# Other step clocks, weights loaded behind x, and small work moved between engines in a one-core S5 and gated-DeltaNet block

## The chip, the cores and the metric

The kernel runs on one core of a Trainium2 chip. Every time is in microseconds (us) of device time for one execution of the whole program. The time of a kernel is the median of its runs. The engines of the core are TensorE (PE, with its weight loads as PEld), VectorE (DVE), ScalarE (ACT), GpSimd (POOL) and SyncE (SP), which issues nearly all DMA transfers. Each works through its own instructions in program order and waits on the others by semaphores.

## The reference

One decoder block for 1024 tokens of width 1024, all in float32:

```
a = rms_norm(h, norm_mix_g)
u_s, z_s, q, k, v, z_d, b_raw, a_raw = split(a @ w_in)
y_s = s5_branch(u_s, ...) * silu(z_s)          # 32 groups, 64 states, gelu, then the GLU:
                                               # y * sigmoid(y @ w_glu + b_glu)
y_d = gated_deltanet_branch(q, k, v, z_d, b_raw, a_raw, ...)
                                               # causal conv of 4 taps + silu on q, k, v;
                                               # l2 norms of q, k; 4 heads of 128, chunks of 64
                                               # g = -exp(A_log) * softplus(a_raw + dt_bias)
h = h + concat(y_s, y_d) @ w_out
e = rms_norm(p @ w_ple_proj, ple_norm_g)
h = h + sigmoid(h @ w_ple_gate) * e
out = rms_norm(h, final_norm_g)
```

The chunk rule solves a unit lower triangular system per chunk and head; the output is the last RMS norm.

## The kernel before

**Products.** A float32 matrix is split into a high and a low part (`hi` is a rounded copy, `lo = raw - hi`, function `split`); a product is three matmuls, hi by hi, hi by lo and lo by hi (`mm3`). The split of a weight is one ScalarE copy (`wh`) and one subtraction, on VectorE for `w_in`'s tiles (`wl`) and by default on GpSimd.

**Stages.** In the prologue the squares of x are taken on ScalarE (`square`) and summed by scans on VectorE (`sumsq`); `rms` is a chain of some fifty small VectorE operations; `scale_x` multiplies the eight row tiles of x by the result. Meanwhile `e_proj` computes the 16 tiles of p @ w_ple_proj (PSUM tile `pe`), which ScalarE evicts to `e`. `xprep` transposes one 128-column slice of half of x on TensorE (`xtp`, four transposes) and evicts it as `ah` (ScalarE) and `al` (VectorE). From then on `inproj` multiplies one weight tile after another by both halves of x (`half`, PSUM tile `pj`, 24 matmuls each). Beside it run the a-chain (`a_prefix`: the prefix sums of the a gate by matmuls against `tg` and `dg`, PSUM tile `pT`, and scans on VectorE), and four batches of S5: `prep` builds `s5x`, TensorE transposes it (`hp`), ScalarE copies that out (`s5h`), TensorE makes the kernels (`kps`), the state injections (`inj`) and, after a scan, the outputs (`yps`). Then come the gate math with the softplus (`g_math`), the transposed v rows (`vtp`, scaled into `vr`), the decay matrices, a forward substitution on VectorE (`subst`), the doubling of the 32-row inverses to 64 (`double`, with `q32`, `d32`, `q64`, `d64`; printed as q and d), the GLU of S5 (`glu`, PSUM tile `pg`; `gr` is y loaded again, `gh` and `gl` its parts), eight chunks of the recurrence (`chunk`, PSUM tile `bk`), and at last the output projection and the gate (`po`, `pq`).

**What sets the order.** TensorE's order is planned by the program itself (the loop behind `fillers`, from line 1419): a clock counts the matmul time issued so far, and each chain (`x_chain`, `a_chain`, `s5_chain` and others) says with a `yield` how much of that clock has to pass before its next step. These numbers stand in the tables `LAT` (line 470) and `PL` (line 1344). Where no chain is due, fillers are issued in the order of the string `FILL`: u, b, q, k, gates, v, z, then the GLU and the outputs. The order on the other engines follows from the same program and the scheduler. Only one raw weight buffer (`wr`) exists, so a weight is loaded when the split of the one before is done. Loads that SyncE issues run one after another from one queue: p and w_ple, x, small tables (`pk`, `wba`, `hb`, `ldt`), and then the weights.

Of the kernel before, what the change touches and what calls it, by code (L numbers as in the profile page):

```python
# [8 lines left out]
F32 = mybir.dt.float32  # L9
# [7 lines left out]
P = 128  # L17
# [8 lines left out]
def hymba_block_kernel(ctx: ExitStack, tc: tile.TileContext, A: dict, out: bass.AP, dbg=None):  # L26
# [149 lines left out]
    xt_ = []  # L176
# [84 lines left out]

    def e_proj(i):
        t, nh = (i % 4, i // 4) if i < 8 else (i // 2, i % 2)
        p = MM("pe")
        for k in range(2):
            (ph, pl), (wh_, wl_) = ew["pt"][k], ew["wp"][k]
            mm3(p, ph[:, csl(t)], pl[:, csl(t)], wh_[:, hsl(nh)], wl_[:, hsl(nh)], k == 0, k == 1)
        yield 0
        if t in (5, 6):
            e = T2("e")  # L270
            act(e, p, AF.Copy)
            SP.dma_start(out=ed[t][:, hsl(nh)], in_=e)
# [11 lines left out]
        xload(i)  # L284
    SP.dma_start(out=pk, in_=A["pk"])
    SP.dma_start(out=wba, in_=A["wba"])

    ah = [T(f"ah{k}", F32R) for k in range(8)]
    al = [T(f"al{k}", F32R) for k in range(8)]

    def xprep(k, hf):
        p = MZ("xtp", [P, 4, P])
        for i in range(4):
            x4 = xt_[4 * hf + i].rearrange("p (c t j) -> p j c t", j=4, c=2)
            tr(p[:, i, :], x4[:, k // 2, k % 2, :], ident)
        hs = hsl(hf)
        g = pk[:, 126 + k:127 + k]
        act(ah[k][:, hs], flat(p), AF.Copy, scale=g)
        return stt(V, al[k][:, hs], flat(p), g, ah[k][:, hs].bitcast(F32), MUL, SUB)

    def scale_x():
        for i in range(8):
            r = ts(V, xt_[i], xt_[i], rinvs[:, i:i + 1], MUL)
        return r

    ctx.enter_context(tc.manual_schedule(engines={mybir.EngineType.PE}))
    e_split("pt", 0)
# [4 lines left out]
        square(i)  # L312
        sumsq(i)
    rms()
    scale_x()
    for i in range(16):
        for _ in e_proj(i):
            pass
# [50 lines left out]
    def s5_params():  # L369
# [98 lines left out]
    kpv = kp.rearrange("h (b j q) t -> b q j h t", j=4, q=2)  # L468

    LAT = dict(  # L470
        prep=14.1, ev=3.3, scan=18.0, tab=6.0, g1=23.0, g2=4.0, dec=14.8, sub=25.0, blk=0.3,
        q32=6.9, d32=8.0, q64=2.0, d64=0.8, kq=4.3, A=1.4, B=4.8, C=1.4, otp=10.3, vtp=23.2, ssq=30.3,
        bs8=11.4, gl=15.1, par=13.8, xp=1.2, sse=1.5, ql=14.0,
    )
    s5t = {}
# [6 lines left out]
    def s5_batch(b):  # L482
# [27 lines left out]
        for ri in range(2):  # L510
# [1 line left out]
            for j in range(4):  # L512
                tr(p[:, j, :], flat(ab[:, ri, j]), ident)
            act(h[:, ri], p, AF.Copy)
        yield LAT["ev"]
        kt = W("x1", "p (q c) -> p q c", c=P)
        kps = [f("kps")[:, 0:P] for f in (MS, MZ)]
        for ri in range(2):
# [79 lines left out]
    def wtile(mt):  # L598
        lo = wp.tile([P, 8, P], F32R, tag="wl", name="wl")
        hi = wp.tile([P, 8, P], F32R, tag="wh", name="wh")  # L600
        raw = raw_w([P, 8, P])
        SP.dma_start(out=raw, in_=A["win"][mt].rearrange("p (k c) -> p k c", k=8))
        split(hi, lo, raw, S, V)
        return hi, lo

    def half(w, hf, evac):
# [151 lines left out]
    def g_math():  # L758
# [40 lines left out]
        lp, lq, l2, lx, lx3, la, lb, lc = (V36()[:, 0:32] for _ in range(8))
        ts(V, lp, ee, 4.527000055531971e-05, MUL)  # L800
        for c in (0.4985410273075104, 6.578732490539551, 29.91191864013672, 60.949668884277344, 57.11296463012695):
            stt(V, lp, lp, c, ee, ADD, MUL)
        ts(V, lp, lp, 20.039552688598633, ADD)
        V.tensor_copy(out=lq, in_=ee)
        for c in (15.062909126281738, 83.04756927490234, 221.7624053955078, 309.0987243652344, 216.42788696289062):
            stt(V, lq, lq, c, ee, ADD, MUL)
        ts(V, lq, lq, 60.11865997314453, ADD)
        V.reciprocal(out=lq, in_=lq)
        tt(V, lp, lp, lq, MUL)
        tt(V, l2, ee, ee, MUL)  # L810
        tt(V, lq, ee, l2, MUL)
        tt(V, lp, lq, lp, MUL)
        stt(V, lp, l2, -0.5, lp, MUL, ADD)
        tt(V, lp, ee, lp, ADD)
        ts(V, lx, ee, 1.0, ADD, 0.5, MUL)
        ts(V, lx, lx, -1.0, ADD)
        tt(V, l2, lx, lx, MUL)
        tt(V, lx3, l2, lx, MUL)
        ts(V, la, lx, 0.07037683576345444, MUL)
        stt(V, la, la, -0.11514610052108765, lx, ADD, MUL)  # L820
        stt(V, la, la, 0.11676998436450958, lx3, ADD, MUL)
        ts(V, lb, lx, -0.12420140951871872, MUL)
        stt(V, lb, lb, 0.14249323308467865, lx, ADD, MUL)
        stt(V, lb, lb, -0.16668057441711426, la, ADD, ADD)
        tt(V, lb, lb, lx3, MUL)
        ts(V, lc, lx, 0.2000071406364441, MUL)
        stt(V, lc, lc, -0.24999994039535522, lx, ADD, MUL)
        stt(V, lc, lc, 0.3333333134651184, lb, ADD, ADD)
        tt(V, lc, lc, lx3, MUL)
        ts(V, lc, lc, -0.00021219444170128554, ADD)  # L830
        stt(V, l2, l2, -0.5, lx, MUL, ADD)
        tt(V, lc, l2, lc, ADD)
        ts(V, lc, lc, 0.693359375, ADD)
        ts(V, la, ee, 0.4142135679721832, ALU.is_lt)
        ts(V, lb, la, -1.0, MUL, 1.0, ADD)
        tt(V, lp, lp, la, MUL)
        tt(V, lc, lc, lb, MUL)
# [117 lines left out]
    def v_tile(h):  # L955
        if not vr:
            vr.extend(T(f"vr{c}", F32, [P, 2, 4, P]) for c in range(4))
        cv = yield from conv_tile(2, h)

        def tail():  # L960
            yield "n"
            for n in range(2):
                p = MMs("vtp", [P, 2, 2, P])
                for i in range(4):
                    tr(p[:, i // 2, i % 2, :], cv[:, csl(4 * n + i)], ident)
                for i in range(2):
                    c = 2 * n + i
                    tt(V, vr[c][:, :, h, :], p[:, i], sq3[:, 2 * c:2 * c + 2, h:h + 1].to_broadcast([P, 2, P]), MUL)
                yield 1.5
            done.add(f"v{h}")  # L970

        later(LAT["vtp"], tail)
# [49 lines left out]
    def glu(hf):  # L1022
        if not wgh:
            for i in range(2):
                wgl.append(wp.tile([P, 2, 512], F32R, tag="wl", name="wgl"))
                wgh.append(wp.tile([P, 2, 512], F32R, tag="wh", name="wgh"))
                raw = TV("wgr", F32, [P, 2, 512])
                SP.dma_start(out=raw, in_=A["wglu"].rearrange("(k p) n -> p k n", p=P)[:, 2 * i:2 * i + 2, :])
                split(wgh[i], wgl[i], raw)
        for c in (2 * hf, 2 * hf + 1):  # L1030
            ysh.append(T(f"ysh{c}", F32R, [P, 2, 4, P]))
            ysl.append(T(f"ysl{c}", F32R, [P, 2, 4, P]))
# [2 lines left out]
        for i in range(2):  # L1035
# [1 line left out]
            for b in range(2):  # L1037
                SP.dma_start(out=raw[:, b], in_=ydv[2 * i + b][:, :, cs])
            v8 = lambda t: t.rearrange("p b (c j) -> p b c j", j=8)
            split(v8(hi), v8(lo), raw.rearrange("p b j c -> p b c j"))  # L1040
            gh += [hi[:, b] for b in range(2)]
            gl += [lo[:, b] for b in range(2)]
        for m in range(4):
# [297 lines left out]
    def later(t, f):  # L1341
        Chain(f(), clock[0] + t)

    PL = dict(
        f0=8.0, x1=26.0, a0=23.9, ca=5.2, s0=34.0, x0=16.7,
    )

    xlast = []
# [1 line left out]
    def x_chain(hf):  # L1350
        for k in range(8):
            xlast.append(xprep(k, hf))
            yield LAT["xp"]
        done.add(f"x{hf}")

    def a_chain():
# [191 lines left out]
```

## Time and profile before

| | |
|---|---|
| median of three runs | 928.14 us (925.67 to 930.21) |
| the profiled execution | 924.7 us, its span 922.9 us |
| mean granted TensorE clock | 0.929 of full speed |
| busy: PE, PEld | 794.8 us (86%), 641.1 us (69%) |
| busy: DVE | 701.2 us (76%) |
| busy: ACT | 491.8 us (53%) |
| busy: POOL | 255.6 us (28%) |

The page counts as busy the time in which an engine works on an instruction. Idle time of TensorE is put down to the instruction that released it, so a wait such as "kps <- ACT s5h" is a place in the program, not a verdict on the engine named. The granted clock says at which of its two levels (1.2 or 2.4 GHz) TensorE ran: a clock of 0.5 in a stretch is the lower one throughout.

### The profile page before, as it was taken

What the parts mean: (1) busy time and instruction counts of PE and PEld (TensorE: products, weight loads), DVE (VectorE), ACT (ScalarE), POOL (GpSimd) and SP (SyncE); (2) the same over time, 40 slices, a digit from 0 to 9 for tenths busy, and PEclk for the clock granted to TensorE, in tenths of its full rate; (3) what the DMA queues carried; (4) which work ended last, traced back from release to release, by engine and by line L of the source; (5) the groups of instructions that cost most, each with busy time, mean ns of one, the idle gap of its engine ahead of it and who ended that gap; (6) DMA issues with size and microseconds to landing.
All of it is one profiled execution on the core that took longest, in us unless ns stands there. A gap on an engine that the chain in (4) does not pass through costs nothing. (4 is left out here: it accounts for less than half of the span.)

```text
span 922.9 us, 12230 instructions
## 1 busy us (share of the span) xinstructions
PE 794.8 (86%) x4338; PEld 641.1 (69%) x4338; DVE 701.2 (76%) x1464; ACT 491.8 (53%) x922; POOL 255.6 (28%) x245
## 2 busy tenths in 40 slices
PE   5469978988697897798889997989989988899996
PEld 3347746866575786686778775868768876678885
DVE  5665896877987969895666898885886687538886
ACT  7436755579666665968757627134442244013443
POOL 0001475440453336230000002025531265502222
PEclk9867988998978999799899999998999998999999
DMA  7340112222220231205110115236570334202211
GB/s 283 137 147 1 46 46 52 69 69 75 68 47 23 75 88 39 86 24 160 69 47 23 45 48 179 72 110 166 137 258 28 115 102 160 92 1 76 85 45 69
DMA packets 67581, 79.93 MB, mean 87 GB/s; under 512 B 23456, under 2 KB 49344, under 8 KB 67520
## 3 DMA queue, kind: packets, MB, share of 16 engines
q1 hardware_dynamic: 67376, 78.89, 26.6%
q8 instruction: 34, 0.56, 0.3%
q14 instruction: 27, 0.22, 0.1%
q10 hardware_dynamic: 144, 0.26, 0.1%
HBM read 57.39 MB, written 21.74 MB: 86 GB/s over the span
## 5 line engine op out<-in xcount | busy, mean ns | idle before, releaser
L115 PE MATMUL pj<-ah,wh 128*128 128x512 f32 x384 | 159.6, 416 | 18.0 <-ACT z L106 5.3
L115 PE MATMUL pj<-ah,wl 128*128 128x512 f32 x384 | 155.5, 405 | 0.0
L115 PE MATMUL pj<-al,wh 128*128 128x512 f32 x384 | 155.5, 405 | 0.0
L106 ACT ACTIVATE F<-F,gridc 128x512 f32<-128x512 f32 x128 | 115.6, 992 | 0.0
L115 PEld LDWEIGHTS pj<-ah,wh 128*128 128x128 f32 x384 | 75.4, 196 | 37.9 <-ACT z L106 6.0
L747 DVE TENSOR_TENSOR_SCAN F<-F,vst 128x192 f32<-128x192 f32 x128 | 85.9, 731 | 11.7 <-ACT F L106 11.6
L747 DVE TENSOR_TENSOR_SCAN F<-F 128x192 f32<-128x192 f32 x128 | 74.1, 639 | 17.5 <-ACT F L106 17.4
L115 PEld LDWEIGHTS pj<-ah,wl 128*128 128x128 f32 x384 | 74.7, 195 | 18.0
L115 PEld LDWEIGHTS pj<-al,wh 128*128 128x128 f32 x384 | 75.2, 196 | 16.2
L95 DVE TENSOR_TENSOR pT<-F 128x512 f32<-128x512 f32 x64 | 49.1, 767 | 43.5 <-ACT F L106 36.0
L115 PE MATMUL pq<-wgl,hth 128*128 128x512 f32 (+1 forms) x200 | 67.0, 387 | 0.0
L115 PE MATMUL pT<-tg,ah 128*128 128x512 f32 x128 | 55.6, 435 | 4.0 <-POOL tg L335 2.1
L727 POOL COPY F<-gridc 128x4 f32<-128x4 f32 x32 | 12.3, 385 | 159.2 <-DVE pT L95 87.4
L106 ACT ACTIVATE F<-pT 128x512 f32<-128x512 f32 x64 | 55.6, 871 | 0.8 <-PE pT L115 0.8
L103 DVE SCALAR_TENSOR_TENSOR cv<-raw,pk,cv 128x1023 f32<-128x1023 f32 (+2 forms) x36 | 49.9, 1386 | 0.1
L95 DVE TENSOR_TENSOR h<-h,po 128x512 f32<-128x512 f32 x32 | 21.9, 686 | 35.0 <-PE po L115 33.6
L95 DVE TENSOR_TENSOR wl<-wr,wh 128x1024 fp32r<-128x1024 f32 x24 | 30.9, 1286 | 20.5 <-ACT wh L106 20.5
L106 ACT ACTIVATE F<-pT,tbl 128x128 f32<-128x128 f32 x128 | 36.8, 385 | 17.7 <-PE pT L115 17.6
L95 POOL TENSOR_TENSOR e<-e,pleg 128x1024 f32<-128x1024 f32 x8 | 19.4, 2430 | 93.6 <-ACT jq L106 84.2
L115 PE MATMUL pT<-dg,ah 128*128 128x512 f32 x128 | 42.6, 416 | 0.5 <-DVE pT L95 0.5
L115 PEld LDWEIGHTS pq<-wgl,hth 128*128 128x128 f32 x200 | 37.0, 188 | 7.4
L727 POOL COPY F<-tbl 128x4 f32<-128x4 f32 x32 | 13.2, 411 | 102.9 <-DVE pT L95 97.0
(330 smaller groups left out, 1988.2 us busy)
## 6 DMA issues: line engine op xcount, KB each, us to landing
wr<-in_win SPq DMA_DIRECT2D x24, 512.0 KB, 3.7
x<-in_x SPq DMA_DIRECT2D x8, 512.0 KB, 7.7
wr<-in_wout SPq DMA_DIRECT2D x8, 512.0 KB, 4.2
h<-in_x SPq DMA_DIRECT2D x8, 512.0 KB, 6.5
wr<-in_wgate SPq DMA_DIRECT2D x8, 512.0 KB, 3.3
e<-ed SPq DMA_DIRECT2D x8, 512.0 KB, 3.2
out<-h SPq DMA_DIRECT2D x7, 512.0 KB, 2.6
ed<-e SPq DMA_DIRECT2D x6, 512.0 KB, 4.7
```

The lines of the kernel that those rows point to most:

```text
L95: return e.tensor_tensor(out=o, in0=a, in1=b, op=op)
L103: return e.scalar_tensor_tensor(out=o, in0=a, scalar=s, in1=b, op0=op0, op1=op1)
L106: return S.activation(out=o, in_=i, func=f, **k)
L115: return PE.matmul(o, lhsT=l, rhs=r, start=a, stop=z, **k)
L727: G.tensor_copy(out=tb[:, :, 0:1], in_=first)
L747: V.tensor_tensor_scan(out=d0, data0=d0, data1=d1, initial=vst[:, i, h:h + 1] if hf else 0.0, op0=ADD, op1=ADD)
```

## The change

- **Tables.** In `LAT`, prep goes from 14.1 to 20, scan from 18 to 22, d32 from 8 to 11, vtp from 23.2 to 28; the step from hp to kps gets a number of its own, 5.0, where it had 3.3. In `PL`, the second half of x starts at 20.5 (26), the a-chain at 20.5 (23.9), S5 at 30 (34). The first half of x is transposed without pauses.
- **Prologue.** The first two weight tiles are loaded directly behind x's small tables, ahead of hb and ldt; the second goes to a tile of its own (`wr2`). Their splits are released only when x3 is scaled. `scale_x` is split: x0 to x3 are scaled ahead of all transposes, x4 to x7 between those of the first half. `e_proj` and the first half's `xprep` also use the three `MX` PSUM buffers, five in all.
- **Softplus.** The branches of the polynomial are written in turns, operation by operation, with three more scratch tiles.
- **v rows.** 16 VectorE products of 128x256 become 32 ScalarE copies of 128x128 with a scale.
- **GLU splits.** The low parts `wgl` and `gl` are made on VectorE instead of GpSimd.

```diff
     def e_proj(i):
-        p = MM("pe")
+        p = (MX if i % 5 % 2 else MM)("pe")
...
+    wfirst = {20: raw_w([P, 8, P]), 21: T("wr2", F32, [P, 8, P])}
+    for mt, raw in wfirst.items():
+        SP.dma_start(out=raw, in_=A["win"][mt].rearrange("p (k c) -> p k c", k=8))
...
     def xprep(k, hf):
-        p = MZ("xtp", [P, 4, P])
+        p = (MX if hf == 0 and k % 5 % 2 else MZ)("xtp", [P, 4, P])
...
-    scale_x()
+    for i in range(4):
+        scale_x(i)
...
-        prep=14.1, ev=3.3, scan=18.0, tab=6.0, g1=23.0, g2=4.0, dec=14.8, sub=25.0, blk=0.3,
-        q32=6.9, d32=8.0, q64=2.0, d64=0.8, kq=4.3, A=1.4, B=4.8, C=1.4, otp=10.3, vtp=23.2, ssq=30.3,
+        prep=20.0, ev=3.3, kps=5.0, scan=22.0, tab=6.0, g1=23.0, g2=4.0, dec=14.8, sub=25.0, blk=0.3,
+        q32=6.9, d32=11.0, q64=2.0, d64=0.8, kq=4.3, A=1.4, B=4.8, C=1.4, otp=10.3, vtp=28.0, ssq=30.3,
...
             act(h[:, ri], p, AF.Copy)
-        yield LAT["ev"]
+        yield LAT["kps"]
...
     def wtile(mt):
-        raw = raw_w([P, 8, P])
-        SP.dma_start(out=raw, in_=A["win"][mt].rearrange("p (k c) -> p k c", k=8))
-        split(hi, lo, raw, S, V)
+        raw = wfirst.pop(mt, None)
+        if raw is None:
+            raw = raw_w([P, 8, P])
+            SP.dma_start(out=raw, in_=A["win"][mt].rearrange("p (k c) -> p k c", k=8))
+        with ExitStack() as st:
+            if mt in (20, 21):
+                gate(st, sx[3])
+            split(hi, lo, raw, S, V)
...
+        def turns(*rows):
+            for i in range(max(map(len, rows))):
+                for r in rows:
+                    if i < len(r):
+                        r[i][0](V, *r[i][1:])
...
+        turns(num, den, large)
...
+        turns(small_, lbs, lcs)
...
-                    tt(V, vr[c][:, :, h, :], p[:, i], sq3[:, 2 * c:2 * c + 2, h:h + 1].to_broadcast([P, 2, P]), MUL)
+                    for j in range(2):
+                        act(vr[c][:, j, h, :], p[:, i, j], AF.Copy, scale=sq3[:, 2 * c + j, h:h + 1])
...
-                split(wgh[i], wgl[i], raw)
+                split(wgh[i], wgl[i], raw, S, V)
...
-            split(v8(hi), v8(lo), raw.rearrange("p b j c -> p b c j"))
+            split(v8(hi), v8(lo), raw.rearrange("p b j c -> p b c j"), S, V)
...
-        f0=8.0, x1=26.0, a0=23.9, ca=5.2, s0=34.0, x0=16.7,
+        f0=8.0, x1=20.5, a0=20.5, ca=5.2, s0=30.0, x0=16.7,
...
     def x_chain(hf):
         for k in range(8):
             xlast.append(xprep(k, hf))
-            yield LAT["xp"]
+            if hf == 0 and k < 4:
+                scale_x(4 + k)
+            yield LAT["xp"] if hf else 0
```

**Where instructions moved.** Three places.

VectorE around the RMS chain, before. `rsc` holds the small values of the chain, `sq` the squares, `wl` the low part of a weight; the last rows scale x.

```order
L192 SCALAR_TENSOR_TENSOR sq<-mask,sq 128x1024
L193 COPY rsc<-sq 128x16
L95 TENSOR_TENSOR wl<-wr,wh 128x1024
L95 TENSOR_TENSOR rsc<-rsc 128x32 x3
...
L95 TENSOR_TENSOR wl<-wr,wh 128x1024
L95 TENSOR_TENSOR rsc<-rsc 128x8 x2
...
L99 TENSOR_SCALAR x_121<-x_121,rsc 128x1024 x2
```

The same place in the changed kernel, from the chain's last row on.

```order
L95 TENSOR_TENSOR rsc<-rsc 128x8
L99 TENSOR_SCALAR x_121<-x_121,rsc 128x1024 x2
L99 TENSOR_SCALAR x_124<-x_124,rsc 128x1024 x2
L95 TENSOR_TENSOR wl<-wr,wh 128x1024
L95 TENSOR_TENSOR wl<-wr_136,wh 128x1024
L99 TENSOR_SCALAR x_127<-x_127,rsc 128x1024 x2
L99 TENSOR_SCALAR x_130<-x_130,rsc 128x1024 x2
```

Both splits stand behind the whole chain and four of x's tiles now; before, one stood ahead of the chain and one inside it.

TensorE between `hp` and `kps` of the second S5 batch, before (the rows left out are the same three matmuls of `pj` for the slices between).

```order
L119 MATMUL hp<-cm,s5x_841 128x128 x8
L115 MATMUL pj<-ah_136,wh 128x512
...
L115 MATMUL pj<-ah_140,wl 128x512
L115 MATMUL pT<-tg_1468,ah_137 128x512
L115 MATMUL pT<-tg_1468,al_145 128x512
...
L115 MATMUL kps<-s5ca,bb 32x128 x16
```

The same place in the changed kernel.

```order
L119 MATMUL hp<-cm,s5x_863 128x128 x8
L115 MATMUL pT<-tg_1458,ah_141 128x512
L115 MATMUL pT<-tg_1458,al_149 128x512
L115 MATMUL pT<-tg_1458,ah_141 128x512
L115 MATMUL pT<-dg_1457,ah_141 128x512 x2
L115 MATMUL pT<-dg_1457,al_149 128x512 x2
L115 MATMUL kps<-s5ca,bb 32x128 x16
```

The 15 matmuls of a projection that stood between the two steps are gone from there; one set of seven for the a-chain is left.

VectorE in the doubling and the GLU in the changed kernel: `em` and `zt` belong to the attention and the doubling, `w` to its 64-row step, `wgl` and `gl` are the GLU's low parts.

```order
L95 TENSOR_TENSOR em_4270<-kq,em_4270 128x512
L95 TENSOR_TENSOR wgl<-wgr,wgh 128x1024
L99 TENSOR_SCALAR zt_3570<-d_4789 32x8x32 x2
...
L99 TENSOR_SCALAR w_4662<-d_4843 32x16x32
L95 TENSOR_TENSOR em_4270<-kq,em_4270 128x512
L95 TENSOR_TENSOR wgl<-wgr,wgh 128x1024
L95 TENSOR_TENSOR em_4284<-kq,em_4284 128x512
...
L99 TENSOR_SCALAR zt_3583<-d_4986 64x8x64
L95 TENSOR_TENSOR gl_5013<-gr,gh_5014 128x1024
L95 TENSOR_TENSOR gl_5020<-gr,gh_5021 128x1024
```

These four splits stood on GpSimd before, where nothing of the doubling ran. On TensorE, the first `pg` group now comes after three of the four `d64` blocks, with no other matmuls behind them.

## Rows read from the trace of the kernel before

**Rows 1.** The page's busy times: us, share of the span, instructions.

```profile
span 922.9 us, 12230 instructions
PE 794.8 (86%) x4338; PEld 641.1 (69%) x4338; DVE 701.2 (76%) x1464; ACT 491.8 (53%) x922; POOL 255.6 (28%) x245
```

**Rows 2.** Windows by stage: the columns, and the stretch of the a-chain and S5.

```profile
core 0: us, PE busy (x) PEld busy (x) DVE busy (x) ACT busy (x) POOL busy (x), PEclk, DMA share, GB/s
92.00:460.00 368.00, 316.53 (x1664) 251.95 (x1663) 300.18 (x468) 256.89 (x469) 136.99 (x162) 0.91 0.22 65
```

**Rows 3.** TensorE's waits, whole run: sum in us, times, longest.

```profile
PE kps L115 <- ACT s5h L106: 10.4, 4, 5.3
...
PE yps L115 <- POOL s5x L95: 7.2, 3, 5.7
...
PE hp L119 <- DVE s5x L95: 4.8, 2, 3.3
```

**Rows 4.** Timeline of TensorE: start, duration, instruction, [idle before <-releaser]; yps of batch two, kps of batch four.

```profile
253.50 0.80 PE L115 MATMUL yps<-s5x,s5ca 64*128 64x127 f32 x4 [5.73 <-POOL s5x L95]
...
371.94 1.49 PE L115 MATMUL kps<-s5ca,bb 64*32 64x128 f32 x32 [7.64 <-POOL F L727]
```

**Rows 5.** Timeline of VectorE in the prologue.

```profile
31.83 2.28 DVE L192 TENSOR_TENSOR_SCAN sq<-mask,sq 128x1024 f32<-128x1024 f32 x1
...
42.68 1.23 DVE L95 TENSOR_TENSOR wl<-wr,wh 128x1024 fp32r<-128x1024 f32 x1 [8.36 <-ACT wh L106]
...
54.16 1.23 DVE L95 TENSOR_TENSOR wl<-wr,wh 128x1024 fp32r<-128x1024 f32 x1 [3.41 <-ACT wh L106]
...
56.37 5.39 DVE L99 TENSOR_SCALAR x<-x,rsc 128x1024 f32<-128x1024 f32 x8
61.68 1.40 DVE L103 SCALAR_TENSOR_TENSOR al<-xtp,pk,ah 128x512 fp32r<-128x512 f32 x2
```

**Rows 6.** Timeline of ScalarE: the first weight's high part.

```profile
41.59 1.06 ACT L106 ACTIVATE wh<-wr 128x1024 fp32r<-128x1024 f32 x1 [9.80 <-DMA wr<-in_win]
```

**Rows 7.** Timeline of TensorE: first transpose, first projection matmul, x's last transposes.

```profile
57.18 0.49 PE L119 MATMUL xtp<-cm,x 128*128 128x128 f32 x1 [4.63 <-DVE x L99]
...
76.62 0.63 PE L115 MATMUL pj<-ah,wh 128*128 128x512 f32 x1
...
85.78 0.64 PE L119 MATMUL xtp<-cm,x 128*128 128x128 f32 x4
```

**Rows 8.** The page's DMA issues: count, KB each, median us to landing.

```profile
wr<-in_win SPq DMA_DIRECT2D x24, 512.0 KB, 3.7
```

**Rows 9.** Timeline of TensorE: two projection matmuls in a row, later on.

```profile
79.70 0.40 PE L115 MATMUL pj<-al,wh 128*128 128x512 f32 x1
79.93 0.40 PE L115 MATMUL pj<-ah,wl 128*128 128x512 f32 x1
```

**Rows 10.** Timeline of VectorE in the softplus: seven in turns, three in a chain.

```profile
538.76 0.80 DVE L103 SCALAR_TENSOR_TENSOR F<-F 128x32 f32<-128x32 f32 x7
...
540.21 0.65 DVE L95 TENSOR_TENSOR F<-F 128x32 f32<-128x32 f32 x3
```

**Rows 11.** v products by tile (min/median/max ns); a ScalarE group by form (sum, mean).

```profile
L95 DVE TENSOR_TENSOR vr<-vtp,sqk x16: 356/414/425, 517.4 to 581.1; 128x256 f32<-128x256 f32 x16
...
L106 ACT ACTIVATE rt<-bk,ex 128x128 f32<-128x128 f32 x28 | 9.3, 366 | 15.5 <-DVE rt L103 15.5
```

**Rows 12.** Timeline of TensorE: a v transpose, and the first d32 block.

```profile
574.89 1.12 PE L119 MATMUL vtp<-cm,cv 128*128 128x128 f32 x4 [6.41 <-ACT z L106]
...
621.80 0.31 PE L115 MATMUL d<-z,qs 32*32 32x32 f32 x2 [3.67 <-DVE qs L1094]
```

**Rows 13.** Timelines of GpSimd, ScalarE and VectorE around the GLU.

```profile
617.69 2.34 POOL L95 TENSOR_TENSOR wgl<-wgr,wgh 128x1024 fp32r<-128x1024 f32 x1 [4.53 <-ACT wgh L106]
...
623.94 1.98 ACT L106 ACTIVATE gh<-gr 128x1024 fp32r<-128x1024 f32 x1 [6.33 <-DMA gr<-yd]
...
650.28 6.05 DVE L95 TENSOR_TENSOR ysl<-sg,ysh 128x256 fp32r<-128x256 f32 x2
```

More of the change, by code (lines that the diff above doesn't have):

```diff
@@ L299, in xprep, with scale_x @@
         return stt(V, al[k][:, hs], flat(p), g, ah[k][:, hs].bitcast(F32), MUL, SUB)
[L301 to L304, printed above, removed]
+    sx = {}
+    def scale_x(i):
+        sx[i] = ts(V, xt_[i], xt_[i], rinvs[:, i:i + 1], MUL)
     ctx.enter_context(tc.manual_schedule(engines={mybir.EngineType.PE}))
@@ L798, in g_math @@
         ee, nea = fq[:, 0:32], fq[:, 32:36]
[L799 to L830, printed above, removed]
@@ L831, in g_math @@
-        stt(V, l2, l2, -0.5, lx, MUL, ADD)
-        tt(V, lc, l2, lc, ADD)
+        lp, lq, l2, lx, lx3, la, lb, lc, l3, lm, ln = (V36()[:, 0:32] for _ in range(11))
+        def turns(*rows):
[3 more added lines that the diff above has]
+                        r[i][0](V, *r[i][1:])
+        num = [(ts, lp, ee, 4.527000055531971e-05, MUL)] + [
+            (stt, lp, lp, c, ee, ADD, MUL)
+            for c in (0.4985410273075104, 6.578732490539551, 29.91191864013672, 60.949668884277344, 57.11296463012695)
+        ] + [(ts, lp, lp, 20.039552688598633, ADD)]
@@ new lines, in g_math @@
+        den = [(lambda e, o, i: e.tensor_copy(out=o, in_=i), lq, ee)] + [
+            (stt, lq, lq, c, ee, ADD, MUL)
+            for c in (15.062909126281738, 83.04756927490234, 221.7624053955078, 309.0987243652344, 216.42788696289062)
+        ] + [(ts, lq, lq, 60.11865997314453, ADD), (lambda e, o, i: e.reciprocal(out=o, in_=i), lq, lq)]
+        large = [
+            (ts, lx, ee, 1.0, ADD, 0.5, MUL), (ts, lx, lx, -1.0, ADD), (tt, l3, lx, lx, MUL), (tt, lx3, l3, lx, MUL),
+            (ts, la, lx, 0.07037683576345444, MUL),
+            (stt, la, la, -0.11514610052108765, lx, ADD, MUL),
+            (stt, la, la, 0.11676998436450958, lx3, ADD, MUL),
+        ]
@@ new lines, in g_math @@
+        turns(num, den, large)
+        small_ = [
+            (tt, lp, lp, lq, MUL), (tt, l2, ee, ee, MUL), (tt, lq, ee, l2, MUL), (tt, lp, lq, lp, MUL),
+            (stt, lp, l2, -0.5, lp, MUL, ADD), (tt, lp, ee, lp, ADD),
+        ]
+        lbs = [
+            (ts, lb, lx, -0.12420140951871872, MUL), (stt, lb, lb, 0.14249323308467865, lx, ADD, MUL),
+            (stt, lb, lb, -0.16668057441711426, la, ADD, ADD), (tt, lb, lb, lx3, MUL),
+        ]
+        lcs = [
+            (ts, lc, lx, 0.2000071406364441, MUL), (stt, lc, lc, -0.24999994039535522, lx, ADD, MUL),
+            (ts, lm, ee, 0.4142135679721832, ALU.is_lt), (ts, ln, lm, -1.0, MUL, 1.0, ADD),
+        ]
@@ L833, in g_math @@
+        turns(small_, lbs, lcs)
+        turns([
+            (stt, lc, lc, 0.3333333134651184, lb, ADD, ADD), (tt, lc, lc, lx3, MUL),
+            (ts, lc, lc, -0.00021219444170128554, ADD),
+        ], [(stt, l3, l3, -0.5, lx, MUL, ADD), (tt, lp, lp, lm, MUL)])
+        tt(V, lc, l3, lc, ADD)
         ts(V, lc, lc, 0.693359375, ADD)
[L834 to L837, printed above, removed]
+        tt(V, lc, lc, ln, MUL)
```

## Prediction

> **What bounds the kernel now.** I read the page's head first: the span is 922.9 us and TensorE is busy for 794.8 of it [rows 1], so some 128 us are its waits, and its half-clock stretches come on top. The windows by stage say where: from 92 to 460 us TensorE is busy for 316.5 of 368 us at a mean clock of 0.91, VectorE for 300.2 of 368 [rows 2]. Neither is full, so this stage is paced by the chain that runs between the engines. The list of what TensorE waited for and its timeline name the places: S5's steps hp, kps and yps take 30.0 us together (4.8, 10.4 + 7.6, 7.2) [rows 3, 4]. The timelines of the prologue give the rest: the first weight's split stands on VectorE ahead of the RMS chain and waits for a late load [rows 5, 6], and TensorE comes to its first projection matmul at 76.6 us only [rows 7].
>
> **Prologue.** Before, the last square-sum scan ends at 34.1 us; then VectorE idles 8.36 us for the first weight's high part and splits it, runs the RMS chain, idles 3.41 us for the second weight, splits that, finishes the chain and scales x from 56.37 us [rows 5]. ScalarE waited 9.80 us for that load alone [rows 6], while a typical weight load lands in 3.7 us [rows 8]. The changed order has no split inside the chain, and the loads directly behind x. The chain itself is 6.9 us (from the end of the first split, 43.9, to 50.8) plus 1.0 (55.4 to 56.4), so x's scaling starts near 34.4 + 7.9 = 42.3. Eight scalings take 5.39 us, 0.67 each [rows 5]: x0 to x3 end at 45.0, two splits of 1.23 at 47.5, x4 to x7 at 50.2, and al follows at 0.70 each [rows 5]. The transposes of the first half need x0 to x3 only, so they start near 45 instead of 57.2 [rows 7]. They have five PSUM tiles instead of two; the eighth set of four reuses the fifth's, which al frees at 53.7, so the first projection matmul falls near 54 instead of 76.6. It has 12 fewer transposes ahead of it, but those come later between matmuls.
>
> A fairer mark is the end of the last transposes of x, at 86.2 [rows 7]. In the new order they stand 13.9 us of full-clock matmul time behind the first projection matmul (0.23 us for each of 128x512 [rows 9]), and by then 3.5 us more work is done. With 2 us for half clock at the start (0.63 against 0.40 us a matmul [rows 7, 9]) and 1.5 us for the gate table's wait, they end at 71.6, and 86.2 + 3.5 - 71.6 = 18.1 us are won. I take **-16**, since ScalarE's twelve late evictions of e stand ahead of ah. The ends are -20 (no wait for the table) and -8 (ScalarE's squares slip behind the loads that now share the queue, and half clock lasts throughout). LDT's small packets and hb are pushed back by two loads of 3.7 us at most [rows 8]; they are read by S5's parameters, which the new table puts later, so I cost that at nothing, or at 2 to 3 us inside the low end if the first gate table's buffer waits for its store behind them. Between 92 and 460 us neither engine is full [rows 2], so the time is kept.
>
> **S5 with more clock.** The table only moves steps among the fillers; what counts is the TensorE work between a step and the one that waits for it (matmuls in the order, at 0.23 us). Ahead of hp there are 8.7 us more: its 4.8 us go. Between hp and kps the four batches had 4.6, 5.0, 5.0 and 5.0 us and get 5.3, **1.6**, 5.8 and 5.8: the second has almost nothing left, as the order shows, because the convolutions that used to stand there wait for other tails. With the needs unchanged, kps waits 3.4 us more in batch two and 0.8 less in each of three and four: +1.8. Between inj and yps they had 18.8, 13.5, 19.0 and 17.6 and get 24.5, 24.8, **13.8** and 25.0. The 13.5 cost 5.73 us [rows 4], so a need of at least 19.2: now batch three waits some 6 where 7.2 were spent in all, -1. The sum is -4.8 + 1.8 - 1 = **-4**. The ends: -20 if the later steps fall where VectorE is free and two thirds of the 30 go; +16 if all four kps need what the worst did, 5.0 + 7.64 = 12.6 [rows 4] (7.3 + 11.0 + 6.8 + 6.8 = 31.9 against 18.0), and yps stays.
>
> **Softplus, v rows.** Operations that stand behind the one they need take 0.22 us each, others 0.11 [rows 10]; written in turns, some 18 change over, 2 us of VectorE. The gate sums' transpose also moves 21 matmuls (4.8 us) forward, and eight v products of 0.41 leave VectorE ahead of it [rows 11]: 2.0 + 3.3 against 4.8, so nothing on the path. For v, 16 products of 0.41 us (6.6) leave VectorE and 32 ScalarE copies come; the trace has none with this input, the nearest are 128x128 evictions with a scale at 0.37 [rows 11], so 11.7 us. ScalarE is half idle, but in the v stage the copies stand between the exps of the decay, and vtp already waits 6.41 us on ScalarE there [rows 12]. I take 0, between -3 (VectorE's products out of the way to the substitution) and +6 (two groups of four copies ahead of the last exp, twice 1.5, each held by the transposes it waits for).
> The table of fixed costs in the Trainium skill, VectorE: DVE Perf Modes, section The TRN2 errata, gives ScalarE 172 + N cycles at 1.2 GHz from PSUM; by that a copy would be 0.25 us and the 32 of them 8.0, an estimate from that page. The row of 0.37 decides. That section's advice against tiles below 512 elements speaks against this part, which cuts 256 into two of 128.
>
> **Double step and GLU.** Before, d waits 3.67 us for the qs copies [rows 12]. The order puts 18 projection matmuls (4.1 us) in front of it: **-4**. The price is paid behind. The GLU's splits move from GpSimd (2.34 us [rows 13]) to VectorE (1.23 us, the same shape [rows 5]), but SyncE's second GLU weight load waits for the first split to free its buffer, that split stands behind the substitution's copies, and the gr loads wait for the second split. Counted from the first split's end: load 3.7, high part 1.06, z and q evictions 0.6 each make 6.0 until d64 can start, with 4.0 us of TensorE work beside it: 2.0 idle. The second split ends at 6.0 and gr arrives 3.9 later (now gh starts at 623.94 after a split that ended at 620.03 [rows 13]), gh takes 1.98, gl 1.23: pg starts at 11.9 and has its second operand at 13.1. TensorE has 2.7 us of d64 work in between, so 3.2 and 1.0 more are idle, 0.2 for the second gl. 6.4 less the 0.6 of now: **+6**, between +2 (the first split runs early) and +14 (gr takes 6, gl as long as on GpSimd). Half clock after this wait is taken as equal to that after d's now.
> The Trainium skill, SBUF — State Buffer, section Who interferes with whom, has it that a VectorE instruction with two SBUF inputs and a GpSimd one that reads SBUF exclude each other. The trace agrees: two ysl took 6.05 us [rows 13] while gl ran on GpSimd. By that rule gl on VectorE would in turn wait for GpSimd's zs products; that is within the +14.
>
> **The sum.** 924.7 (the profiled execution; its span is 922.9) - 16 - 4 + 0 - 4 + 6 = 906.7. That execution lies 3.4 us under the median of 928.14 and 1.0 under the lowest of three; a new median should stand between 0 and 3.4 above the sum, so **908**, -2.2%.
>
> **Rivals.** *S5's clock works*: the steps fall where queues are empty, the waits of kps and yps go, 910.7 - 20 + 1 = **892**. For it: VectorE has 68 us free in that stage [rows 2]. Against: kps waits for ScalarE and GpSimd queues [rows 3, 4], not for VectorE, and its cover hardly grows. *S5's change does not do what it says*: fewer matmuls in front of the second kps and the third yps starve TensorE, all kps at the worst need, 910.7 + 16 - 5 (a third of it hidden by steps that run earlier) = **922**; the prologue is then all that is left. *The late stages lose more than all else wins*, the slower side: ScalarE's and VectorE's queues run in order, so v copies, splits and exps hold each other; GLU +14, v +6, and two waits that put TensorE at half clock for some 10 us each (5 lost, 0.63 us a matmul against 0.40): +30 less the 4 of d, with nothing from S5: 924.7 - 16 + 26 = **935**. It decides once these waits pass 21 us together. For it: the loads that wait for splits. Against: GpSimd's slower splits are off that path.
>
> **How the numbers follow.** Forecast (about 900 to 917) 0.53, S5 works 0.15, S5 fails 0.18, late stages 0.09, and 0.05 for a prologue of only -8. A measurement can tell about 0.5% from no change, which puts the bounds at 923.5 and 932.8. Faster takes the first two, most of the prologue case and two fifths of the third: 0.78; same gets the rest of these: 0.13; slower 0.09. The range that leaves out 2 in 10 goes from 892 to 927.
>
> **What would show it.** Right: x's scaling at 42 to 45, the first projection matmul at 52 to 58, no hp wait, a kps wait of 5 to 8 us in batch two and a yps wait near 6 in batch three, no wait of d, and 5 to 9 us at d64 and the first pg. Wrong: x's scaling after 50, kps waits gone in all batches, q32 waiting instead of d, or vtp waits that sum to over 12 us.

## The result and the profile after

The changed kernel takes 915.2 us (median of 4 runs, 914.3 to 916.7) against 926.9 us (923.6 to 930.2) for the kernel before, run beside it on the same chip. The ratio is 0.988, with a 95% interval of 0.985 to 0.991: 11.7 us, or 1.2%, faster. The forecast was 908 with a range of 892 to 927. The profiled execution took 914.6 us, its span 912.9. The total came out 7 us worse than forecast, and two of the large terms in it were far off, in opposite directions.

The page's head after, for [rows 1]:

```profile
PE 790.6 (87%) x4338; PEld 644.0 (71%) x4338; DVE 696.1 (76%) x1454; ACT 499.8 (55%) x954; POOL 242.0 (27%) x239
```

The windows by stage (start:end and length, then each engine's busy time with its instructions, the granted TensorE clock, the DMA share). The second row answers [rows 2]:

```profile
0.00:92.00 92.00, 66.64 (x293) 54.22 (x294) 66.61 (x164) 64.03 (x87) 8.08 (x27) 0.93 0.44 150
92.00:460.00 368.00, 316.71 (x1694) 254.94 (x1693) 299.09 (x455) 254.75 (x470) 136.10 (x156) 0.91 0.23 66
```

What TensorE waited for (in all, times, longest), for [rows 3]:

```profile
PE ssp L115 <- ACT z L106: 12.3, 2, 9.5
PE pT L115 <- ACT F L106: 11.4, 5, 4.8
PE po L115 <- DVE h L95: 8.8, 3, 5.7
PE bk L115 <- ACT rt L106: 7.0, 8, 2.1
PE vtp L119 <- ACT z L106: 6.5, 1, 6.5
PE pab L115 <- ACT ut L106: 6.4, 1, 6.4
PE inj L115 <- DMA s5u<-ud: 5.1, 1, 5.1
```

The waits of hp and yps are gone and d waits no more; kps keeps 2.7, all of it in batch two. But in the S5 stage TensorE is as busy as before, 316.7 of 368 us at a clock of 0.91: waits of the squares' sums, of the a-chain and of `pab` stand there now.

VectorE in the prologue after, for [rows 5], and TensorE, for [rows 7]:

```profile
35.39 0.32 DVE L193 COPY rsc<-sq 128x16 f32<-128x16 f32 x3
43.80 2.74 DVE L99 TENSOR_SCALAR x<-x,rsc 128x1024 f32<-128x1024 f32 x4
46.45 2.36 DVE L95 TENSOR_TENSOR wl<-wr,wh 128x1024 fp32r<-128x1024 f32 x2
...
55.83 0.48 PE L115 MATMUL pj<-ah,wh 128*128 128x512 f32 x1
71.36 0.64 PE L119 MATMUL xtp<-cm,x 128*128 128x128 f32 x4
```

This is as the prediction had it: x's scaling at 43.8, the first projection matmul at 55.8, the last transposes of x at an end of 72.0 (71.6 was worked out).

**A common measure.** The order on TensorE differs between these kernels, so marks such as "the first vtp" do not compare them. I added up the matmuls in the order in which they ran, each at its full-clock time (0.23 us for 128x512, 0.11 for a 128x128 transpose, less for the small ones; 692 us for the whole kernel), and read when each profiled execution had done the same sum. The table gives how many us earlier than the kernel before it stood there. The columns are the end of the prologue (60 us of work), the a-chain and S5 nearly done (330), ahead of the double step (435), behind it (465), the GLU done (495), and the end. The columns 60, 330 and the end change by less than 2 us whatever price the small matmuls are given. The double step, with its many small ones, lies between 435 and 495, and the columns 435 and 465 shift by several us with that price (the row with S5's numbers back most of all), so they are a rough guide.

| us ahead of before at work | 60 | 330 | 435 | 465 | 495 | end |
|---|---|---|---|---|---|---|
| changed kernel | 17.8 | 20.2 | 11.9 | 12.3 | 6.9 | 10.0 |
| GLU splits on GpSimd again | 18.5 | 17.5 | 9.1 | 2.7 | -6.3 | -3.1 |
| v rows on VectorE again | 18.6 | 20.9 | 14.2 | 10.1 | 4.2 | 7.4 |
| S5's numbers back | 17.8 | 10.9 | 7.2 | 0.3 | -12.8 | -14.9 |
| the same, gate sums in place | 17.9 | 10.8 | 3.4 | 6.3 | 0.1 | 3.3 |
| prologue alone | 17.3 | 10.4 | 13.9 | -7.3 | -8.5 | -12.5 |
| the same, gate sums in place | 18.4 | 11.5 | 8.8 | 5.1 | 4.7 | 3.8 |
| changed kernel, g1 at 15 | 18.4 | 18.7 | 7.6 | 4.7 | 4.9 | 16.0 |

### The profile page after: what moved, and what is told of

It reads as the page before. It is cut to its first block, busy times and chain, and to the rows that moved or that the text cites. A ratio compares the mean times of both kernels' runs of the same rounds, so it can differ in the third digit from the quotient of the medians.

```text
span 912.9 us, 12256 instructions
## 1 busy us (share of the span) xinstructions
PE 790.6 (87%) x4338; PEld 644.0 (71%) x4338; DVE 696.1 (76%) x1454; ACT 499.8 (55%) x954; POOL 242.0 (27%) x239
## 5 line engine op out<-in xcount | busy, mean ns | idle before, releaser
L756 DVE TENSOR_TENSOR_SCAN F<-F,vst 128x192 f32<-128x192 f32 x128 | 86.9, 740 | 12.5 <-ACT F L106 12.4
L756 DVE TENSOR_TENSOR_SCAN F<-F 128x192 f32<-128x192 f32 x128 | 75.6, 646 | 10.6 <-ACT F L106 10.4
L103 DVE SCALAR_TENSOR_TENSOR cv<-raw,pk,cv 128x1023 f32<-128x1023 f32 (+2 forms) x36 | 46.4, 1289 | 0.1
L115 PEld LDWEIGHTS pT<-tg,ah 128*128 128x128 f32 x128 | 25.8, 202 | 23.8 <-ACT F L106 13.4
```

Of the source, the lines that this page charges most:

```text
L103: return e.scalar_tensor_tensor(out=o, in0=a, scalar=s, in1=b, op0=op0, op1=op1)
L115: return PE.matmul(o, lhsT=l, rhs=r, start=a, stop=z, **k)
L756: V.tensor_tensor_scan(out=d0, data0=d0, data1=d1, initial=vst[:, i, h:h + 1] if hf else 0.0, op0=ADD, op1=ADD)
```

## The experiments

**One part undone at a time.** First the v rows, the GLU splits and the softplus.

```diff
-                    for j in range(2):
-                        act(vr[c][:, j, h, :], p[:, i, j], AF.Copy, scale=sq3[:, 2 * c + j, h:h + 1])
+                    tt(V, vr[c][:, :, h, :], p[:, i], sq3[:, 2 * c:2 * c + 2, h:h + 1].to_broadcast([P, 2, P]), MUL)
```

> The changed kernel with the v rows scaled by VectorE again (16 products of 128x256), all else as changed. Theory A: the copies on ScalarE are what costs the lead at the v transposes, since the second transposes of each tile, a projection behind them and one half-clock spell of 6.8 us wait for them; without them vtp's 1.89 and pj's 1.84 go, with half of the spell, so some 6 us less than the changed kernel: about 909. Rival B: the later place of the transposes (28 in the table instead of 23.2) makes the loss and not the engine: no change, 914 to 916. Rival C: VectorE's products stand ahead of the gate sums or the substitution and push them back by up to 16 x 0.41 = 6.6: up to 921.

Measured: 917.2 us (5 runs), ratio to the kernel before 0.988 (0.986 to 0.990), which the changed kernel's interval covers. The v rows' place on ScalarE costs 4 us at the transposes (18.0 against 13.9 us ahead at a work of 375), so A's mechanism is there, but the gain is lost again by a work of 495. B's time holds (by the ratio), not its reason. Where the gain goes, this execution shows TensorE at half clock from 607.9 to 631.8 us:

```profile
607.90:631.80 23.90, 23.26 (x161) 20.13 (x161) 10.53 (x13) 7.86 (x8) 7.23 (x4) 0.50 0.60 155
```

The changed kernel is at half clock for only about 10 us around the same work (608.6 to 612.0 and 622.3 to 629.1). No run shows whether the v rows bring that spell about. The copies of the changed kernel, eight in a row:

```profile
499.67 2.25 ACT L106 ACTIVATE vr<-vtp,sqk 128x128 f32<-128x128 f32 x8
```

```diff
-                split(wgh[i], wgl[i], raw, S, V)
+                split(wgh[i], wgl[i], raw)
...
-            split(v8(hi), v8(lo), raw.rearrange("p b j c -> p b c j"), S, V)
+            split(v8(hi), v8(lo), raw.rearrange("p b j c -> p b c j"))
```

> The changed kernel with the low parts of the GLU's weights and of y made on GpSimd again. Theory A, as the prediction had it: VectorE's in-order queue pushes the splits behind the substitution's copies, which costs 6 us at d64 and the first pg; without it about 909. Rival B: GpSimd's slower split (2.34 against 1.0 us) and two ysl of 6 us come back and cost as much: 914 to 917. Rival C: what TensorE loses behind the double step comes from the order (d32 11 instead of 8) and not from the engine of the splits: no change.

Measured: 926.7 us (12 runs), ratio 0.999 (0.997 to 1.001): 11.5 us slower than the changed kernel. All three theories fall, and with them the prediction's sign. TensorE does the same work in the same order in both; the first products of the GLU in the changed kernel:

```profile
621.11 0.50 PE L115 MATMUL pg<-gh,wgh 128*128 128x512 f32 x1 [0.53 <-ACT gh L106]
623.20 0.79 PE L115 MATMUL pg<-gl,wgh 128*128 128x512 f32 x1 [1.59 <-DVE gl L95]
```

and in this run, where `gl` comes from GpSimd:

```profile
632.78 0.80 PE L115 MATMUL pg<-gl,wgh 128*128 128x512 f32 x1 [0.98 <-POOL gl L95]
```

The GLU starts 10 us later, and not all of that is the splits' own time. In these two executions 2.9 us stand already at q's products (600.38 against 597.51), ahead of all that the edit changes. Most of the rest lies in a spell of half clock. The stretch from the `kq` products that wait for `w` to the first product with `gl` is the same work in both; it took 14.33 us in the changed kernel, at a mean clock of 0.86, and 20.08 us in this run, at 0.50 throughout:

```profile
608.87:623.20 14.33, 12.21 (x141) 10.66 (x141) 9.48 (x14) 7.76 (x8) 0.00 (x0) 0.86 0.65 175
612.70:632.78 20.08, 19.11 (x140) 17.05 (x140) 6.36 (x11) 7.75 (x8) 5.25 (x3) 0.50 0.50 131
```

The run above with the v rows on VectorE had a spell of half clock there too, with the splits on VectorE, so the spell is not shown to come from GpSimd. What the trace shows of GpSimd itself is smaller: `gl` took 2.86 us there against 1.92 on VectorE, and while GpSimd made `wgl`, VectorE's copies into `w` took 3.80 us, in this run:

```profile
602.86 3.80 DVE L1102 COPY w<-q 32x512 f32<-32x512 f32 x4
```

and 1.70 in the changed kernel:

```profile
599.99 1.70 DVE L1102 COPY w<-q 32x512 f32<-32x512 f32 x4
```

One of the four copies took 2.52 us, the other three some 0.41 each, as all four do in the changed kernel.

The softplus was written branch by branch again:

```diff
-        turns(num, den, large)
-        turns(small_, lbs, lcs)
+        ts(V, lp, ee, 4.527000055531971e-05, MUL)
+        for c in (0.4985410273075104, 6.578732490539551, 29.91191864013672, 60.949668884277344, 57.11296463012695):
+            stt(V, lp, lp, c, ee, ADD, MUL)
...
```

> The changed kernel with the softplus written branch by branch again. Theory A: VectorE then needs some 2 us more for the gate math, but in the changed kernel the gate sums are ready 8 us before their transpose comes in TensorE's order, so nothing changes: within 1.5 us of 915. Rival B: those 2 us reach the exps of the decay and the substitution through VectorE's queue: 917.

Measured: 913.7 us (4 runs), ratio 0.985 (0.983 to 0.986), overlapping the changed kernel's interval. A holds. The reason is in the changed kernel's trace: the gate sums (`gg`) end at 522.8, VectorE then idles for 7.3 us, and their transpose comes in TensorE's order only at 531.

```profile
522.64 0.19 DVE L95 TENSOR_TENSOR gg<-F 128x32 f32<-128x32 f32 x1
530.12 1.23 DVE L95 TENSOR_TENSOR wl<-wr,wh 128x1024 fp32r<-128x1024 f32 x1 [7.29 <-ACT wh L106]
...
531.16 0.27 PE L119 MATMUL gtp<-cm,gg 128*32 128x128 f32 x1
```

**The prologue alone**, all else as before (v rows, GLU splits, softplus, `LAT`, and s0 at 34; only x1 and a0 at 20.5).

```diff
-        f0=8.0, x1=26.0, a0=23.9, ca=5.2, s0=34.0, x0=16.7,
+        f0=8.0, x1=20.5, a0=20.5, ca=5.2, s0=34.0, x0=16.7,
```

> The prologue's part alone: the kernel before, with the two weights loaded behind x, x's scaling in two halves, five buffers and the first half of x without pauses (so with x1 and a0 at 20.5), the S5 and attention numbers and all other operations as before. Theory A: the prologue gives 16 to 18 us and keeps them, as the sum had it: 909 to 911. Rival B: a lead of this size is lost on the way at places where something other than TensorE sets the pace (loads, ScalarE's queue), and the changed kernel's late losses come from the lead itself: 914 to 918. Rival C: it only holds with the changed S5 numbers: 918 to 924.

Measured: 935.8 us (6 runs), ratio 1.008 (1.006 to 1.010): some 8 us *slower* than before, which no theory had. The lead is there (17.3 us), 7 of it go in the S5 stage, and some 21 between a work of 435 and 465, in one wait:

```profile
555.75 0.28 PE L119 MATMUL gtp<-cm,gg 128*32 128x128 f32 x1
...
625.26 3.63 PE L115 MATMUL q<-q,zt 32*32 32x32 f32 x128 [19.95 <-DVE q L1080]
```

q needs the substitution on VectorE, and the substitution starts from the gate sums. So I counted the matmuls between the transpose of the gate sums (`gtp`) and q. The windows from `gtp` to q have that count behind PE's busy time. The kernel before:

```profile
550.00:614.80 64.80, 58.01 (x265) 46.80 (x264) 54.63 (x120) 24.34 (x36) 9.76 (x7) 0.95 0.32 108
```

The changed kernel:

```profile
531.10:597.50 66.40, 57.86 (x265) 46.01 (x263) 55.54 (x115) 27.91 (x51) 7.99 (x6) 0.95 0.31 111
```

The prologue alone:

```profile
555.70:625.20 69.50, 44.85 (x209) 35.90 (x207) 62.85 (x114) 26.93 (x35) 20.58 (x12) 0.84 0.42 129
```

There are 265, 265 and 209. Here the gate sums stand 12 us of work later (404 against 392), the projections run out, and q comes while the substitution is still running. It is also slow: 36.7 us on VectorE, against 30.8 in the kernel before, with single steps stretched while GpSimd makes a low part for the GLU (added up, its 62 steps take 32.6 us here and 21.2 there):

```profile
596.26 2.40 POOL L95 TENSOR_TENSOR wgl<-wgr,wgh 128x1024 fp32r<-128x1024 f32 x1 [12.04 <-ACT wgh L106]
...
595.68 0.42 DVE L95 TENSOR_TENSOR q<-q,xt 128x255 f32<-128x255 f32 x1
596.02 0.68 DVE L95 TENSOR_TENSOR em<-kq,em 128x512 f32<-128x512 f32 x1
596.62 2.31 DVE L95 TENSOR_TENSOR xt<-q,q 128x256 f32<-128x256 f32 x1
598.97 0.42 DVE L95 TENSOR_TENSOR q<-q,xt 128x256 f32<-128x256 f32 x1
```

Two suspects, then: the place of the gate sums, and the GLU's splits. Three runs tell them apart. First, the prologue with the GLU's splits on VectorE (the reverse of the GLU diff above):

> The prologue's part and the GLU's low parts on VectorE, nothing else of the change. The prologue-alone run keeps a lead of 13.9 us until TensorE has done 435 us of work and loses 24.5 in the next 15, in a wait of 20 us for the substitution on VectorE, which took 36.7 us (584.8 to 621.5). Theory A: it was stretched by the GLU's GpSimd instructions that ran at the same moments (VectorE steps of 0.4 us took 2.3 to 2.9); without them it takes some 28 and this run gives 912 to 918. Rival B, the prediction's reading: VectorE's queue is what these splits load, and they cost 6 us: 940. Rival C: the wait comes from the order of the double step (d32 at 8, not 11): 930 to 936, q still waits.

Measured: 930.9 us (12 runs), ratio 1.004 (1.002 to 1.006). Rival C holds: q still waits.

```profile
618.27 3.62 PE L115 MATMUL q<-q,zt 32*32 32x32 f32 x128 [20.66 <-DVE q L1080]
```

GpSimd's splits no longer stretch the substitution, but the same splits now stand within it in VectorE's queue, and it ends at about the same distance from its start, 34.5 us. The splits' engine is worth 4 to 5 us in this order, and is not the cause of the wait.

Second, holding the GpSimd splits back:

```diff
+        act(hi, raw, AF.Copy)
+        with ExitStack() as st:
+            gate(st, sublast[-1])
+            tt(G, lo, raw, hi.bitcast(F32), SUB)
```

> The prologue-alone kernel with its GLU low parts still on GpSimd and in the same order on every engine, but each held until the substitution's last step. Theory A (they stretch it by running beside it): the substitution takes 26 to 28 us instead of 36.7 and q's wait shrinks from 20 to some 10; the splits then come late, so pg waits and the time falls by less, to 925 to 932. Rival B: the substitution is slow for another reason, such as its own place behind kq's products: still 36 us, q waits 20 or more, and the time rises to 938 or more.

Measured: 934.3 us (4 runs), ratio 1.008 (1.006 to 1.011). The edit did nothing: `gate` only sets an order among instructions, which was already this one, and the first split still ran in the middle of the substitution, as this run's row shows.

```profile
594.58 2.50 POOL L95 TENSOR_TENSOR wgl<-wgr,wgh 128x1024 fp32r<-128x1024 f32 x1 [11.25 <-ACT wgh L106]
```

It decides nothing, but as a second measurement of the prologue alone it gives nearly the same time and the same 20.5 us at q.

Third, the prologue alone with the gate sums brought forward, so that 265 matmuls stand between them and q again:

```diff
-        prep=14.1, ev=3.3, kps=3.3, scan=18.0, tab=6.0, g1=23.0, g2=4.0, dec=14.8, sub=25.0, blk=0.3,
+        prep=14.1, ev=3.3, kps=3.3, scan=18.0, tab=6.0, g1=12.0, g2=4.0, dec=14.8, sub=25.0, blk=0.3,
```

> The prologue alone with one more number: g1 at 12 instead of 23, which puts the transpose of the gate sums back to its distance from q's products in the kernel before (265 matmuls between them there, 210 in the prologue-alone run). Theory A: that run lost its lead since the gate sums came late among the projections, which then ran out before the substitution was done; in place, q's wait of 20 us goes, the lead of 10.4 us that it has at 330 us of TensorE work is kept, and the time is 915 to 918. Rival B: the substitution is held back by VectorE's and GpSimd's other work, wherever the transpose stands: q still waits over 10, 928 or more. Rival C: the GLU's GpSimd splits now meet the substitution's end and the double step as in the run with these splits back on GpSimd, which lost 11 us: about 927.

Measured: 924.0 us (12 runs), ratio 0.998 (0.995 to 1.001), some 11 us less than the prologue alone by one number. q's wait falls from 20 to 3.2 us. So A's cause of q's wait is right; its time (915 to 918) is not, since only 3.8 of the 11.5 us that the lead had at a work of 330 reach the end. The time lies nearer to C's 927, and what C names is in the trace: GpSimd's `wgl` meets the substitution's end and the copies into `w`, where one VectorE step takes 2.36 us and one copy 2.48. It cannot be all, since the run below with S5's numbers back and the gate sums in place has its splits on VectorE and loses as much (10.8 to 3.3).

**S5's numbers back**, all else as changed.

```diff
-        prep=20.0, ev=3.3, kps=5.0, scan=22.0, tab=6.0, g1=23.0, g2=4.0, dec=14.8, sub=25.0, blk=0.3,
+        prep=14.1, ev=3.3, kps=3.3, scan=18.0, tab=6.0, g1=23.0, g2=4.0, dec=14.8, sub=25.0, blk=0.3,
...
-        f0=8.0, x1=20.5, a0=20.5, ca=5.2, s0=30.0, x0=16.7,
+        f0=8.0, x1=20.5, a0=20.5, ca=5.2, s0=34.0, x0=16.7,
```

> The changed kernel with S5's steps at their former distances (prep 14.1, kps 3.3, scan 18, S5 started at 34), all else as changed. Theory A: the new distances are worth what separates the changed kernel from the prologue-alone run when TensorE has done 330 us of work, before any late stage: 9.8 us; so about 924, with hp, kps and yps waits back. Rival B, the prediction's term of -4: 919. Rival C: what is lost in S5 is hidden by later waits: 914 to 917.

Measured: 937.0 us (6 runs), ratio 1.010 (1.007 to 1.013): S5's numbers are worth 20 to 22 us in the changed kernel, not 4. A names 9.8 of them; the rest appears behind a work of 330. TensorE's waits in this run:

```profile
PE pj L115 <- DVE ssq L919: 10.5, 2, 7.5
PE q L115 <- DVE q L1086: 10.2, 1, 10.2
PE kps L115 <- ACT s5h L106: 9.8, 2, 7.2
...
PE pj L115 <- DVE ssk L919: 5.5, 1, 5.5
...
PE hp L119 <- DVE s5x L95: 4.6, 1, 4.6
PE yps L115 <- POOL s5x L95: 4.3, 2, 3.6
```

Again q waits, with 232 matmuls between the gate sums and it. So the same number (g1 at 10.6 instead of 23) was changed here:

> The changed kernel with S5's steps at their former distances, but g1 at 10.6, so that the gate sums stand where the changed kernel has them relative to q's products. Theory A: of the 22 us that the former distances cost, 9.8 are S5's own waits and the rest is the late place of the gate sums: about 924 to 926, with no wait of q. Rival B: all of it is lost in S5 and what follows from it: 935 or more. Rival C: nearly all of it is the place of the gate sums: 915 to 918.

Measured: 924.8 us (12 runs), ratio 0.998 (0.995 to 1.000), and no wait of q in the trace. A holds: of the 22 us some 12 were the place of the gate sums, which g1 alone gives back, and some 10 are S5's own.

**The GLU's splits alone**, on the kernel before.

> The kernel before with only the GLU's low parts moved to VectorE. Theory A (GpSimd's splits stretch what VectorE does beside them): in the kernel before only the copies into w (3.80 us, where the changed kernel has 1.70) were hit, and gl takes 5.7 on GpSimd, so a few us less: 921 to 925. Rival B, the prediction's term of +6: 931 to 933. Rival C: no path runs through these splits here: 926 to 928.

Measured: 928.6 us (12 runs), ratio 1.003 (1.001 to 1.005), a loss of 2 to 3 us. A and B fall, and C (no path runs through the splits) comes nearest. So the same edit loses 2 to 3 us on the kernel before, wins 4 to 5 on the prologue alone, and wins 11.5 in the full change.

**Gate sums earlier in the changed kernel.** Its gate sums are ready 8.3 us ahead of their transpose, so g1 was set to 15:

> The changed kernel with g1 at 15 instead of 23, which puts the transpose of the gate sums some 8 us of TensorE work earlier; the sums are ready 8.5 us before it now, and VectorE idles 7.3 us there. Theory A: gate math, substitution and the eight chunks start earlier while more projections are left to cover them, so the late waits (vtp 6.5, po on h 8, bk on rt 7) shrink: 906 to 912. Rival B: the chunks then run out of GLU and output work at another place, or the v rows' ScalarE copies hold the decay's exps: 915 to 920.

Measured: 908.9 us (6 runs), ratio 0.981 (0.977 to 0.985), 6 us less than the changed kernel; A holds. The transpose now follows the gate sums closely and q waits a little, as this run's timeline shows:

```profile
523.75 0.28 PE L119 MATMUL gtp<-cm,gg 128*32 128x128 f32 x1
593.08 3.62 PE L115 MATMUL q<-q,zt 32*32 32x32 f32 x128 [5.80 <-DVE q L1086]
```

268 matmuls stand between the two here, more than the 265 that were enough in the changed kernel, and still q waits: the substitution takes 33.2 us from its first to its last step, against 28.0 there, with 7.3 us of idle time within it against 3.0. So the count alone does not settle the wait. The late waits shrink; its list of waits, to be set beside the 7.0 and 8.8 above:

```profile
PE bk L115 <- ACT rt L106: 3.7, 4, 1.9
PE po L115 <- DVE h L95: 3.4, 3, 1.9
```

The last run put 16 matmuls in front of q on top of it (sub at 30 instead of 25):

> The changed kernel with g1 at 15 and the distance from the decay to q's products (sub) at 30 instead of 25. With g1 at 15 alone q waits 5.8 us for the substitution; this puts some 16 matmuls (3.7 us) in front of it. Theory A: the wait shrinks to about 2 and nothing else moves: 3 to 4 us under the 908.9 of that run. Rival B: the eight chunks move back by the same amount and lose cover among the GLU's products, so the 3.7 us come back there: 907 to 911. Rival C: kq or the first pg now waits instead: 911 or more.

Measured: 908.6 us (6 runs), ratio 0.980 (0.977 to 0.983). No difference, as rival B had it. q's wait fell from 5.8 to 1.6 us, and the chunks' waits for `rt` rose from 3.7 to 7.9:

```profile
PE bk L115 <- ACT rt L106: 7.9, 6, 3.2
```

## Why the prediction was right, and where it was not

- **The prologue, -16.** The mechanism and the size hold up to the end of the prologue: 17.8 us ahead at a work of 60. What failed is the sentence that carried the gain to the end, "neither engine is full, so the time is kept". Alone, the part ends some 8 us slower than before. TensorE's share of busy time does not say whether the order behind a gain can use it: with the old numbers the lead shrank to 10.4 us in the S5 stage, and in that order the a-chain, though started earlier, ends 8 us of work later than before, and the gate sums stand 12 us of work later.
- **S5, -4.** This term is off by 16 to 18 us, and the value lay near the end of its range (-20) and of the rival "S5's clock works". The step that failed is "the table only moves steps among the fillers". I counted only the cover of hp, kps and yps. About 10 us are S5's own (9.4 us of lead at a work of 330), more than the 4 of the count: hp lost its wait as forecast, but kps keeps 2.7 us in batch two, where 5 to 8 were forecast, and yps waits in no batch, where some 6 were forecast in the third; instead the `pT` ahead of the second kps waits, and a group of square sums (`ssp`, 9.5 us) ahead of the third batch. The other 12 us are not waits of S5 at all. The a-chain and the gate math run on the same clock, so the numbers of S5 also set how many matmuls are left between the gate sums and q: 265 in the changed kernel and 232 with S5's old numbers in it. The orders of the kernel before and of the changed kernel could not show this, since both have 265; it takes the order with one part undone.
- **The GLU's splits, +6.** Wrong in sign. I priced what the splits cost in VectorE's queue: at d64 and the first pg TensorE waits some 4 us where 5 to 9 were forecast, and moved alone they lose 2 to 3 us. I left out what GpSimd's version costs: some 2 us for each VectorE step that it blocks, and 2.86 us for each `gl`. The row for it was in the trace before: the 2.34 us of `wgl` [rows 13] lie beside the copies of the kernel before, which take 1.70 in the changed one, and the last of the four takes 2.51:

```profile
616.50 3.80 DVE L1087 COPY w<-q 32x512 f32<-32x512 f32 x4
...
617.79 2.51 DVE L1087 COPY w<-q 32x512 f32<-32x512 f32 x1
```

  The size, 11.5 us, holds only in the changed kernel's order, and these costs do not add up to it: the half clock described above came with it. The rule that the prediction cited from the Trainium skill, SBUF — State Buffer, section Who interferes with whom, agrees with the substitution's steps: VectorE's step of 2.31 us ends 0.3 us behind GpSimd's instruction. The copies into `w` have one input, so that rule does not speak of them, and the trace shows one stretched all the same. I had applied the rule to the few zs products and not to the splits that leave GpSimd.
- **d, -4.** Right: the wait [rows 12] is gone, and the lead grows by 5.8 us there. By a work of 495 that gain is lost again.
- **Softplus and v rows, 0.** Right in size; neither can be told from nothing (913.7 and 917.2 against 915.2). For v a loss of 4 us at the transposes is real; why it does not reach the end stays open, as said above. A copy lasts 0.38 us, as the row of 0.37 [rows 11] had it, but copies in a row overlap and start 0.25 us apart (8 in 2.25), so the 32 keep ScalarE busy for 9.0 us and not 11.7. The Trainium skill's 0.25 (VectorE: DVE Perf Modes, The TRN2 errata) is that distance.
- **The sum.** -18 was forecast and -11.7 came. It came near because errors cancel: the prologue, forecast at -16, is some +8 alone, and the other parts, forecast at -2 together, take some 20 us off that (935.8 to 915.2). Undone one at a time, S5 and the GLU cost over 20 and 11.5 us, more than that; such numbers do not add up; a likely reason is that both mend the same stretch between the gate sums and the GLU. The 7 us that are missing lie behind a work of 330, where the lead falls from 20.2 to 10.0; with g1 at 15 about 6 come back, behind a work of 495, so most of them hang on where the gate sums' transpose stands, which the prediction had settled with "nothing on the path".

What stays open: why, with the gate sums in place, the lead of the prologue alone still falls from 11.5 to 3.8 us, and how much of the GLU's 11.5 us is GpSimd's blocking, how much its slower `gl`, and how much a longer spell of half clock that may have another cause. No run separated these: the one meant for it did not hold the splits. S5's new numbers were not run alone on the kernel before.

## What to carry to other kernels

Where one clock plans all chains, a number that delays one chain moves every later chain against the stock of independent matmuls. Count, in the order, the matmuls between the start of a serial chain and its consumer, before and after, for every chain on that clock and not only for the one that is named, and set beside it how long the chain itself takes. Price an operation that changes engines on both: what it adds to the new queue, and what it did to the other engine's instructions where it ran.

## What was unexpected of the hardware

- A GpSimd subtraction of 128x1024 (2.3 to 2.5 us) that overlaps VectorE's small two-input steps stretches one of them to its own length: 2.31 us instead of 0.42. GpSimd's own time hardly changed (2.40 against 2.34). A copy of 32x512 with one input was stretched in the same way, 2.51 us instead of 0.42.
- VectorE's `gl`, 128x1024 through a rearranged view, took 1.9 us while GpSimd was idle, against 1.23 for `wl` of the same shape [rows 5], which I had used as its price. The row is of the prologue with the GLU's splits:

```profile
605.10 1.92 DVE L95 TENSOR_TENSOR gl<-gr,gh 128x1024 fp32r<-128x1024 f32 x1 [1.33 <-ACT gh L106]
```
